# Low parts of a third of the early weight chunks by accumulating transfers, and 128-column causal matmuls in the attention

## The chip, the core and the metric

The kernel runs on one core of a Trainium2 chip. The metric is the device time of one execution in microseconds (us). The kernel before was run three times: the median is 706.12 us, the lowest 705.9 and the highest 706.37. One further execution was profiled; it took 705.1 us.

## The reference, cut to what matters

The program is a decoder trunk of two layers on 256 tokens with a model width of 1024, all in float32. In each layer one projection gives the attention's q, k, v and gate, an indexer's q, k and head weights, the input and gate of a recurrence, and two merge gates. The indexer's scores pick 64 causal keys for each query, and softmax attention runs over these.

```python
h = rmsnorm(x, norm_g[l])
proj = h @ w_in[l]
q, k, v, ga, iq, ik, iw, xr, gr, ma, mb = jnp.split(proj, offsets, axis=-1)
...
dots = jnp.einsum('bqhd,bsd->bqhs', iqb, ik)               # indexer
idx_score = jnp.einsum('bqh,bqhs->bqs', iwb, jax.nn.relu(dots))
idx_score = jnp.where(causal[None], idx_score, -jnp.inf)
_, sel = lax.top_k(idx_score, topk)
...
logits = jnp.einsum('bqhd,bqkhd->bhqk', qb, k_sel) * scale  # attention over the kept keys
p = jax.nn.softmax(jnp.where(valid[:, None], logits, -jnp.inf), axis=-1)
attn = jnp.einsum('bhqk,bqkhd->bqhd', p, v_sel)
y_a = (attn * jax.nn.silu(ga)) @ w_out_attn[l]
y_b = (hr * jax.nn.silu(gr)) @ w_out_rnn[l]                 # hr: the recurrence
x = x + (jax.nn.sigmoid(ma) * y_a + jax.nn.sigmoid(mb) * y_b) @ w_o[l]
```

A query attends to no key behind it, so for the first 128 queries only the first 128 keys count.

## The kernel before

The time is in the weights. All of them stand in one stream of 128x128 blocks in the order in which they are used; eight blocks make a chunk of 128x1024 numbers (512 KB), and 224 chunks are loaded as `raw` and two half chunks as `rah`, all from SyncE's queue. TensorE multiplies in fp32r, a format that holds fewer bits than float32, so every weight is split: `wh` is the chunk rounded to fp32r, `wl` is what the rounding lost, `raw - wh`. The activations are split alike (`hh` and `hl`), and `mm3` does three matmuls for each block: high by high, low by high, high by low. A chunk therefore makes 24 matmuls of 256 columns, or 12 of 512 where a projection is laid out by token (`v`, `ma`, `mb`, `yb`, `ya`). `wh` is a copy on ScalarE or, where the planner puts it there, on VectorE; `wl` is always a subtraction on VectorE (`chunk`, L556 to L572; the recorded line is that of the helpers `copy`, L480 and L482, and `sub`, L486). There are 4 buffers for `raw` and 6 pairs of `wh` and `wl`.

The order on each engine is not that of the code. `plan` lists the units of a layer in the order of the weight stream: the indexer's queries, then the recurrence with the light projections between, then for each pair of heads q, k, (v for four heads) and `attn`, then `yb`, `ya` and the output. Every operation is recorded with an estimated duration, and `Program.issue` then runs a simulated clock over all of them: for each engine `choose` takes the operation that can start first, and of several the one with the lowest priority number. On TensorE that number is the place in the recorded order plus a delay (`late`), so the indexer's `dots` and the attention's logits (`lg`), transposes (`ptp`) and products with v (`av`) are pushed behind later projections and fill in between their matmuls. On the other engines it is a due time that is counted back from TensorE's order. What comes out is fixed: each engine works through its list in order and waits at semaphores.

In the attention two blocks of 128 queries are handled as t = 0 and 1. `dots` (L876) and `logits` (L1082) let all matmuls run over 256 keys, though for t = 0 only the first 128 are read afterwards. `attend` (L1107) turns the three causal 128x128 blocks of the softmax weights, puts them behind 128 columns of zeros in `pth` and `ptl`, and multiplies with v: for both blocks of keys 256 columns, of which half are those zeros for the second block. `self.vt` holds the split v of four heads; it is made anew for the second four.

Of the kernel before, what the change touches and what calls it, by code (L numbers as in the profile page):

```python
# [20 lines left out]
L = 2  # L21
# [43 lines left out]
def plan(l):  # L65

    u = [("head",)]
    iq = [("iq", i) for i in range(8)]
    light = []
    for n, i in (("ga", 0), ("mb", 0), ("ga", 1), ("mb", 1), ("ga", 2), ("ma", 0), ("ga", 3), ("ma", 1)):  # L70
        light += [(n, 2 * i), (n, 2 * i + 1)] if n == "ga" else [(n, i, c) for c in range(4)]
    u += iq[3:NRAW]
    for i in range(NRAW, 8):
        u += light[:NMIX] + [iq[i]]
        light = light[NMIX:]
    for j in range(KR):
        u += [("xr", j), ("gr", j)]
        u += light[:2 if j % 3 == 0 else 1]
        light = light[2 if j % 3 == 0 else 1:]
        if j >= DELAY:  # L80
            u.append(("gate", j - DELAY))
    for j in range(KR - DELAY, KR):
        u += light[:2]
        light = light[2:]
        u.append(("gate", j))
    u += light
    for pr in range(4):
        u += [("q", 2 * pr), ("q", 2 * pr + 1), ("k", 2 * pr), ("k", 2 * pr + 1)]
        if pr % 2 == 0:
            u += [("v", pr // 2, c) for c in range(4)]  # L90
        u.append(("attn", pr))
    u += [("yb", n) for n in range(2)]
    if l == L - 1:
        return u + [("xt", 0), ("ya", 0), ("xt", 1), ("ya", 1), ("wt", 0), ("wt", 1)]
    u += [("ya", n) for n in range(2)]
    return (u + [("wo", m, 0, 4) for m in range(6)] + [("wo", m, 4, 8) for m in range(6)]
            + [("wo", m, 0, 8) for m in range(6, 8)])
# [48 lines left out]

NBLK = sum(len(unit_blocks(u)) for l in range(L) for u in plan(l))
NCH = -(-NBLK // 8)


class H:
# [57 lines left out]
def real(a):  # L209
    return a.ap() if isinstance(a, V) else a  # L210
# [12 lines left out]
TABS[AF.Sqrt] = ("sqrt",)  # L223
TABS[AF.Sin] = ("sin",)
PSUM_TAGS = ("pp", "pq", "pt")
ENGINES = ("pe", "act", "dve", "pool", "dma")
LATENCY = {"pe": 190.0, "act": 140.0, "dve": 130.0, "pool": 200.0, "dma": 2000.0}
TO_PE = 230.0
SWITCH = 1283.0

# [1 line left out]
class Program:  # L232
# [52 lines left out]
    def issue(self):  # L285
# [24 lines left out]
        for o in ops:  # L310
            if not o.need:
                enter(o)
        table = None
        order = []
        n = 0
        total = len(ops)
        pepos = 0.0
        while n < total:
# [19 lines left out]
            for h in o.new:  # L338
                k = (h.pool, h.tag)
                slots[k].pop(0)  # L340
                given[k][h.index] = True
                while nalloc[k] < len(given[k]) and given[k][nalloc[k]]:
                    nalloc[k] += 1
            o.start, o.end = s, s + cost
            free[o.eng] = o.end
            if o.eng == "pe":
# [47 lines left out]
    def choose(self, e, cand, free, slots, nalloc, given, table, pepos):  # L394

        best = None
        now = free[e]
        for o in cand:
            s = max(now, o.ready)
            if e != o.eng and max(free[o.eng], o.ready) < s + GAIN:  # L400
                continue
            ok = True
            for h in o.new:
                k = (h.pool, h.tag)
                fr = slots[k]
                ahead = min(h.index - sum(given[k][nalloc[k]:h.index]) - nalloc[k], KEEP.get(h.tag, 1000))
                if len(fr) <= ahead:
                    ok = False
                    break
                s = max(s, fr[0])  # L410
            if not ok:
                continue
            pr = o.prio[0]
            if e == "act" and o.tabs is not ANY and table not in o.tabs:
                pr += TABLE_LAG
                if o.prio[0] > pepos + URGENT:
                    s = max(s, o.ready + HOLD)
            key = (s if s > now else now, pr, o.no)
            if best is None or key < best[0]:
                best = (key, s, o)  # L420
        return None if best is None else (best[1], best[2])
# [2 lines left out]
RING = ("pp", "pq", "pt", "wh", "wl", "raw", "lt0", "lt1", "f2", "mx", "m8")  # L424
KEEP = {"r2": 6, "f1": 5, "f2": 1}
TABLE_LAG = 10000.0
URGENT = 8000.0
HOLD = 0.0
GAIN = 500.0
# [3 lines left out]
def trunk(ctx, tc, xT, pos, pre, par, fgb, wst, out):  # L433
# [78 lines left out]
              lambda: nc.tensor.matmul(real(o), real(w), real(m), start=start, stop=stop, skip_group_check=grp))  # L512

    def trans(o, i):
        pg.op("pe", 70, [o], [i, ident], lambda: nc.tensor.transpose(real(o), real(i), real(ident)))

    def load(o, src, cost, beside=False):

# [9 lines left out]
    class Stream:  # L528
# [23 lines left out]
        def chunk(self, c):  # L552
            if c not in self.parts:
# [11 lines left out]
                    return self.parts[c]  # L565
                wh = pg.tile(wp, "wh", [P, 1024], F32R, nm("wh"), WBUF)
                wl = pg.tile(wp, "wl", [P, 1024], F32R, nm("wl"), WBUF)
                copy(wh, raw)
                sub(wl, raw, wh.bitcast(F32))
                pg.shift = 0.0  # L570
                self.parts[c] = (wh, wl)
            return self.parts[c]  # L572
# [58 lines left out]
    pg.op("pool", 500, [ident], [], lambda: make_identity(nc, real(ident)))  # L631
    pts = []
    for i in range(2):
        ph = const(f"pth{i}", [512], F32R)
        pl = const(f"ptl{i}", [512], F32R)
        pset(ph.bitcast(F32)[:, 0:128], 0.0)
        pset(pl.bitcast(F32)[:, 0:128], 0.0)
        pts.append((ph, pl))

    def mm3(o, rhs, first, last, grp=False):  # L640
        wh, wl = ws.block()
# [143 lines left out]
    class Layer:  # L785
        def __init__(self, l, xg, norm):
# [4 lines left out]
            self.sga, self.sma, self.smb = {}, {}, {}  # L791
            self.xc, self.xs, self.rix, self.sy, self.g = {}, {}, {}, {}, {}
            self.rope = {}
            self.aT = []
            self.m = []
            self.banks = {}
# [74 lines left out]
        def dots(self, i, st, t):  # L871

            pg.late = LATE_DOTS
            ps = bank("pq", "dots")
            for a in range(2):
                w = st[a][:, t * P:t * P + P]  # L876
                mm(ps[:, a, :], w, self.kh, True, False)
                mm(ps[:, a, :], w, self.kl, False, True)
            pg.late = 0.0
            n = P * (t + 1)  # L880
            o = self.wk[t]
            rl = f2("rl")
            act(rl[:, :, :n], ps[:, :, :n], AF.Relu)
# [183 lines left out]
        def v(self, n, c):  # L1067
            ps = self.by_token("v", self.h[2 * c:2 * c + 2], c == 0, c == 3)
            if c == 3:
                self.vt = []  # L1070
                for t in range(2):
                    self.vt.append((r2("vh").join(), r2("vl").join()))
                    split(self.vt[t], ps[t])

        def attn(self, pr):
            pg.late = LATE_LOG
# [5 lines left out]
        def logits(self, hd):  # L1082
# [1 line left out]
            a = hd % 2  # L1084
            ps = bank("pq", "lg")
            for t in range(2):
                s = slice(t * P, t * P + P)
                mm(ps[:, t, :], qh[:, a, s], kh[:, a, :], True, False)
                mm(ps[:, t, :], qh[:, a, s], kl[:, a, :], False, False)
                mm(ps[:, t, :], ql[:, a, s], kh[:, a, :], False, True)  # L1090
            lts = []
            for t in range(2):
                n = P * (t + 1)
# [14 lines left out]
        def attend(self, hd, lts):  # L1108
            pg.late = LATE_LOG + LATE_TURN
            ps = bank("pt", "ptp").join()  # L1110
            for dst, lt, s in ((384, 1, 0), (128, 1, P), (256, 0, 0)):
                trans(ps[:, dst:dst + P], lts[lt][:, s:s + P])
            ph, pl = pts[hd % 2]
            act(ph[:, P:], ps[:, P:], AF.Copy)
            sub(pl[:, P:], ps[:, P:], ph.bitcast(F32)[:, P:])
            a = hd % 4
            pg.late = LATE_LOG + 2 * LATE_TURN
            ps = bank("pt", "av")[:, 0, :]
            n = 0
            for st in range(2):  # L1120
                vh, vl = self.vt[st]
                r = slice(256 - 256 * st, 512 - 256 * st)
                c = slice(a * P, a * P + P)
                for w, m in ((vh, ph), (vh, pl), (vl, ph)):
                    mm(ps, w[:, c], m[:, r], n == 0, n == 5)
                    n += 1
            of = f1("of")
            mul(of, ps, self.sga[hd])
# [191 lines left out]
```

## Time and profile before

| | |
|---|---|
| median of three runs | 706.12 us |
| the profiled execution | 705.1 us, of which its span 703.3 us |
| TensorE matmuls busy | 686.1 us (98%), 4720 instructions |
| VectorE busy | 602.6 us (86%) |
| ScalarE busy | 482.8 us (69%) |
| transfers of the weight queue | 124.44 MB, 56.5% of the 16 DMA engines' time |

All times below are of the one profiled execution and count from the start of its span. TensorE pipelines its matmuls: the duration of a row runs to the end of the last result and covers the next matmul's start, so a busy TensorE may still be slower than it could be. Its pace is the distance between the starts of two rows that follow each other. A number in brackets at a row's end is time in which the engine sat idle before it, with what ended that.

### The profile page before, as it was taken

To read this page: it belongs to the slowest core of one execution; us is meant where nothing else is said; L and a number is where in the kernel's file an instruction comes from. 1 tells how busy PE (TensorE), PEld (TensorE's weight loads), DVE (VectorE), ACT (ScalarE), POOL (GpSimd) and SP (SyncE) were. 2 spreads that over 40 slices of the span, in tenths; PEclk is the share of its full clock that TensorE was granted. 3 is DMA by queue.
4 is the path that set the end of the run, shared out by engine and by line. 5 is a ranking of instruction groups with operands and counts; after the bars stand their busy time and mean duration, and the time that the engine had idled before them with its cause. 6 is when DMAs were issued, how large, how long until landed. Compare 5 with 4: busy or idle time off the path is not lost.

```text
span 703.3 us, 12628 instructions
## 1 busy us (share of the span) xinstructions
PE 686.1 (98%) x4720; PEld 638.4 (91%) x4720; DVE 602.6 (86%) x1177; ACT 482.8 (69%) x775; POOL 6.4 (1%) x18
## 2 busy tenths in 40 slices
PE   7898999999999999999999999999999999999996
PEld 7898999999999998888999899999999898988885
DVE  7989999999897959857779997999989987796573
ACT  7996675799995748444558766588769765674433
POOL 0000000000000000000000000000000000000000
PEclk9999999999999999999999999999999999999999
DMA  8646566667756462655553655576666565535621
GB/s 292 195 157 211 159 197 201 203 189 220 223 177 189 149 192 75 205 180 179 173 173 111 213 178 163 177 220 207 210 205 185 182 190 163 180 101 171 195 73 60
DMA packets 38104, 125.24 MB, mean 178 GB/s; under 512 B 4892, under 2 KB 7260, under 8 KB 38044
## 3 DMA queue, kind: packets, MB, share of 16 engines
q1 hardware_dynamic: 38044, 124.44, 56.5%
q8 instruction: 37, 0.61, 0.3%
q14 instruction: 23, 0.19, 0.1%
HBM read 119.77 MB, written 1.05 MB: 172 GB/s over the span
## 4 chain that ended last, share of the span: by engine, by line
PE 82%; DVE 7%; ACT 6%; issue 2%; DMA 2%; SPq 0%; DVEq 0%; ACTq 0%
PE rps L512 14%; PE yb L512 9%; PE q L512 7%; PE k L512 7%; PE ops L512 6%; PE ma L512 6%; PE ya L512 6%; PE v L512 6%; PE gps L512 5%; PE ga L512 4%; PE mb L512 4%; DVE wl L486 2%; PE iq L512 2%; ACT wh L480 2%; PE lg L512 2%
## 5 line engine op out<-in xcount | busy, mean ns | idle before, releaser
L486 DVE TENSOR_TENSOR wl<-raw,wh 128x1024 fp32r<-128x1024 f32 x223 | 271.5, 1220 | 58.4 <-ACT wh L480 57.1
L480 ACT ACTIVATE wh<-raw 128x1024 fp32r<-128x1024 f32 x196 | 207.3, 1059 | 138.6 <-PE rps L512 21.4
L512 PE MATMUL rps<-hh,wh 128*128 128x256 f32 x352 | 99.5, 283 | 0.0
L512 PE MATMUL rps<-hl,wh 128*128 128x256 f32 x352 | 99.5, 283 | 0.0
L512 PE MATMUL rps<-hh,wl 128*128 128x256 f32 x352 | 99.5, 283 | 0.0
L512 PEld LDWEIGHTS rps<-hh,wl 128*128 128x128 f32 x352 | 67.4, 192 | 0.3
L512 PEld LDWEIGHTS rps<-hh,wh 128*128 128x128 f32 x352 | 67.3, 191 | 0.3
L512 PEld LDWEIGHTS rps<-hl,wh 128*128 128x128 f32 x352 | 67.4, 191 | 0.0
L512 PE MATMUL yb<-wh,g 128*128 128x512 f32 x176 | 59.0, 396 | 0.0
L512 PE MATMUL iq<-xg,wh 128*128 128x256 f32 x232 | 45.3, 285 | 0.0
L512 PE MATMUL ya<-wh,aT 128*128 128x512 f32 x128 | 40.8, 395 | 0.0
L512 PE MATMUL ga<-hh,wh 128*128 128x256 f32 x128 | 36.3, 283 | 2.0 <-DVE iwt L486 2.0
L512 PEld LDWEIGHTS iq<-xg,wh 128*128 128x128 f32 x232 | 37.4, 192 | 0.0
L512 PEld LDWEIGHTS yb<-wh,g 128*128 128x128 f32 x176 | 32.5, 188 | 5.3
L512 PE MATMUL q<-hh,wl 128*128 128x256 f32 x128 | 36.4, 284 | 0.0
L512 PE MATMUL q<-hh,wh 128*128 128x256 f32 x128 | 36.3, 284 | 0.0
L512 PE MATMUL ga<-hl,wh 128*128 128x256 f32 x128 | 36.3, 283 | 0.0
L512 PE MATMUL k<-hh,wl 128*128 128x256 f32 x128 | 36.3, 283 | 0.0
L512 PE MATMUL q<-hl,wh 128*128 128x256 f32 x128 | 36.2, 283 | 0.0
L512 PE MATMUL ga<-hh,wl 128*128 128x256 f32 x128 | 36.2, 283 | 0.0
L512 PE MATMUL k<-hh,wh 128*128 128x256 f32 x128 | 36.2, 283 | 0.0
L512 PE MATMUL k<-hl,wh 128*128 128x256 f32 x128 | 36.2, 283 | 0.0
(264 smaller groups left out, 1944.6 us busy)
## 6 DMA issues: line engine op xcount, KB each, us to landing
raw<-in_wst_dram SPq DMA_DIRECT2D x224, 512.0 KB, 4.0
xk<-xs SPq DMA_DIRECT2D x24, 48.0 KB, 3.5
out_dram<-z SPq DMA_DIRECT2D x4, 256.0 KB, 2.3
rah<-in_wst_dram SPq DMA_DIRECT2D x2, 256.0 KB
xr<-in_xT_dram SPq DMA_DIRECT2D x1, 512.0 KB
fg<-in_fgb_dram SPq DMA_DIRECT2D x2, 256.0 KB
xk<-xs SPq DMA_DIRECT2D x8, 40.0 KB
xf<-xs SPq DMA_DIRECT2D x2, 160.0 KB
```

Source lines behind the costliest of these rows:

```text
L480: lambda: nc.scalar.activation(real(o), real(i), AF.Copy),
L486: lambda: nc.vector.tensor_tensor(real(o), real(a), real(b), op=op))
L512: lambda: nc.tensor.matmul(real(o), real(w), real(m), start=start, stop=stop, skip_group_check=grp))
```

## The change

Two things are changed, and the planner's numbers with them. First, chunks 6, 9, 12 and so on of the stretch of each layer that lies ahead of the q projections (`SUMMED`, 38 chunks in all) get their `wl` in another way: ScalarE writes minus the rounded chunk into `wl`, and a transfer that GpSimd issues adds the chunk to it from HBM. `wh` is copied as before, and `raw` is still loaded. Second, for t = 0 the matmuls of `dots` and `logits` run over 128 keys, and in `attend` the second block of keys takes 128 columns; the zeros and the four instructions that set them go. That makes 160 matmuls narrower: 64 `dots`, 48 `lg` and 48 `av`. In the planner a matmul cannot take less than `ISSUE` unless wider ones ahead of it have left something over (`spare`), narrow ones are held back until there is, and a transpose is given a larger cost. The v projection of heads 4 to 7 is moved ahead, between the q and k projections of the second pair.

```diff
--- before.py
+++ after.py
@@ -86,8 +86,10 @@
         u += [("q", 2 * pr), ("q", 2 * pr + 1), ("k", 2 * pr), ("k", 2 * pr + 1)]
-        if pr % 2 == 0:
-            u += [("v", pr // 2, c) for c in range(4)]
+        if pr == 0:
+            u += [("v", 0, c) for c in range(4)]
+        if pr == 1:
+            u[-4:] = [w for c, w in enumerate(u[-4:]) for w in (("v", 1, c), w)]
         u.append(("attn", pr))
@@ -148,6 +150,20 @@
+def summed_chunks():
+    out, n = set(), 0
+    for l in range(L):
+        early = sum(len(unit_blocks(u)) for u in plan(l)[:plan(l).index(("q", 0))])
+        out.update(range(n // 8 + 6, (n + early) // 8, 3))
+        n += sum(len(unit_blocks(u)) for u in plan(l))
+    return out
+SUMMED = summed_chunks()
@@ -223,8 +239,8 @@
 PSUM_TAGS = ("pp", "pq", "pt")
-ENGINES = ("pe", "act", "dve", "pool", "dma")
-LATENCY = {"pe": 190.0, "act": 140.0, "dve": 130.0, "pool": 200.0, "dma": 2000.0}
+ENGINES = ("pe", "act", "dve", "pool", "dma", "sum")
+LATENCY = {"pe": 190.0, "act": 140.0, "dve": 130.0, "pool": 200.0, "dma": 2000.0, "sum": 3500.0}
 TO_PE = 230.0
@@ -341,6 +358,9 @@
                     nalloc[k] += 1
+            if o.eng == "pe":
+                cost = max(cost, ISSUE - self.spare)
+                self.spare = min(max(self.spare + cost - ISSUE, 0.0), SPARE)
             o.start, o.end = s, s + cost
@@ -415,6 +435,8 @@
                     s = max(s, o.ready + HOLD)
+            if e == "pe" and o.cost < ISSUE:
+                pr += -SHORT if self.spare >= ISSUE - o.cost - 5.0 else SHORT
             key = (s if s > now else now, pr, o.no)
@@ -424,6 +446,9 @@
 TABLE_LAG = 10000.0
+ISSUE = 110.0
+SPARE = 60.0
+SHORT = 6000.0
 URGENT = 8000.0
@@ -512,7 +537,7 @@
     def trans(o, i):
-        pg.op("pe", 70, [o], [i, ident], lambda: nc.tensor.transpose(real(o), real(i), real(ident)))
+        pg.op("pe", 112, [o], [i, ident], lambda: nc.tensor.transpose(real(o), real(i), real(ident)))
@@ -565,8 +590,15 @@
                 wl = pg.tile(wp, "wl", [P, 1024], F32R, nm("wl"), WBUF)
-                copy(wh, raw)
-                sub(wl, raw, wh.bitcast(F32))
+                if c in SUMMED:
+                    pg.op("act", 94 + 0.833 * 1024, [wl], [raw],
+                          lambda: nc.scalar.activation(real(wl), real(raw), AF.Copy, scale=-1.0))
+                    copy(wh, raw)
+                    pg.op("sum", 2000, [wl], [wl],
+                          lambda: nc.gpsimd.dma_start(real(wl), wst[c], accum_op=OP.add))
+                else:
+                    copy(wh, raw)
+                    sub(wl, raw, wh.bitcast(F32))
                 pg.shift = 0.0
@@ -631,11 +663,7 @@
     for i in range(2):
-        ph = const(f"pth{i}", [512], F32R)
-        pl = const(f"ptl{i}", [512], F32R)
-        pset(ph.bitcast(F32)[:, 0:128], 0.0)
-        pset(pl.bitcast(F32)[:, 0:128], 0.0)
-        pts.append((ph, pl))
+        pts.append((const(f"pth{i}", [384], F32R), const(f"ptl{i}", [384], F32R)))
@@ -872,12 +901,12 @@
             ps = bank("pq", "dots")
+            n = P * (t + 1)
             for a in range(2):
                 w = st[a][:, t * P:t * P + P]
-                mm(ps[:, a, :], w, self.kh, True, False)
-                mm(ps[:, a, :], w, self.kl, False, True)
+                mm(ps[:, a, :n], w, self.kh[:, :n], True, False)
+                mm(ps[:, a, :n], w, self.kl[:, :n], False, True)
             pg.late = 0.0
-            n = P * (t + 1)
             o = self.wk[t]
@@ -1067,10 +1096,9 @@
             if c == 3:
-                self.vt = []
+                self.vt[n] = [(r2("vh").join(), r2("vl").join()) for _ in range(2)]
                 for t in range(2):
-                    self.vt.append((r2("vh").join(), r2("vl").join()))
-                    split(self.vt[t], ps[t])
+                    split(self.vt[n][t], ps[t])
@@ -1084,10 +1112,10 @@
             for t in range(2):
-                s = slice(t * P, t * P + P)
-                mm(ps[:, t, :], qh[:, a, s], kh[:, a, :], True, False)
-                mm(ps[:, t, :], qh[:, a, s], kl[:, a, :], False, False)
-                mm(ps[:, t, :], ql[:, a, s], kh[:, a, :], False, True)
+                s, n = slice(t * P, t * P + P), P * (t + 1)
+                mm(ps[:, t, :n], qh[:, a, s], kh[:, a, :n], True, False)
+                mm(ps[:, t, :n], qh[:, a, s], kl[:, a, :n], False, False)
+                mm(ps[:, t, :n], ql[:, a, s], kh[:, a, :n], False, True)
             lts = []
@@ -1108,21 +1136,21 @@
             ps = bank("pt", "ptp").join()
-            for dst, lt, s in ((384, 1, 0), (128, 1, P), (256, 0, 0)):
+            for dst, lt, s in ((2 * P, 1, 0), (0, 1, P), (P, 0, 0)):
                 trans(ps[:, dst:dst + P], lts[lt][:, s:s + P])
+            ps = ps[:, :3 * P]
             ph, pl = pts[hd % 2]
-            act(ph[:, P:], ps[:, P:], AF.Copy)
-            sub(pl[:, P:], ps[:, P:], ph.bitcast(F32)[:, P:])
+            act(ph, ps, AF.Copy)
+            sub(pl, ps, ph.bitcast(F32))
             a = hd % 4
             n = 0
-            for st in range(2):
-                vh, vl = self.vt[st]
-                r = slice(256 - 256 * st, 512 - 256 * st)
+            for st, r in ((0, slice(P, 3 * P)), (1, slice(0, P))):
+                vh, vl = self.vt[hd // 4][st]
                 c = slice(a * P, a * P + P)
                 for w, m in ((vh, ph), (vh, pl), (vl, ph)):
-                    mm(ps, w[:, c], m[:, r], n == 0, n == 5)
+                    mm(ps[:, st * P:], w[:, c], m[:, r], n == 0, n == 5)
                     n += 1
```

VectorE, in the first 25 us, from the scaled unit matrices of the norm (`dg`) on; `wl` and `wh` are the parts of weight chunks, `ang` and `kk` belong to the rotary tables, `hf` to the normed input. Before:

```order
L501 TENSOR_SCALAR dg_267<-ident_76,sd_234 128x128
L501 TENSOR_SCALAR kk_270<-ang_258 128x256
L486 TENSOR_TENSOR wl_277<-raw_207,wh_253 128x1024
L501 TENSOR_SCALAR kk_270<-kk_270 128x256
L486 TENSOR_TENSOR wl_293<-raw_225,wh_274 128x1024
L505 SCALAR_TENSOR_TENSOR ang_258<-kk_270,ang_258 128x256
L486 TENSOR_TENSOR wl_316<-raw_240,wh_296 128x1024
L505 SCALAR_TENSOR_TENSOR ang_258<-kk_270,ang_258 128x256
L486 TENSOR_TENSOR wl_339<-raw_264,wh_319 128x1024
L505 SCALAR_TENSOR_TENSOR ang_258<-kk_270,ang_258 128x256
L505 SCALAR_TENSOR_TENSOR hf_362<-head_72,rstd_305 128x256
L505 SCALAR_TENSOR_TENSOR ang_258<-kk_270,ang_258 128x256
```

and in the changed kernel:

```order
L526 TENSOR_SCALAR dg_259<-ident_76,sd_226 128x128
L526 TENSOR_SCALAR kk_262<-ang_250 128x256
L507 CAST wh_268<-raw_217 128x1024
L511 TENSOR_TENSOR wl_275<-raw_199,wh_245 128x1024
L526 TENSOR_SCALAR kk_262<-kk_262 128x256
L530 SCALAR_TENSOR_TENSOR ang_250<-kk_262,ang_250 128x256 x2
L511 TENSOR_TENSOR wl_310<-raw_232,wh_288 128x1024
L530 SCALAR_TENSOR_TENSOR ang_250<-kk_262,ang_250 128x256
L511 TENSOR_TENSOR wl_333<-raw_256,wh_313 128x1024
L530 SCALAR_TENSOR_TENSOR ang_250<-kk_262,ang_250 128x256
```

The chunk that was `raw_225` is now `raw_217`: VectorE copies its high part (`CAST`) and has no subtraction for it; its low part is row 22 of ScalarE and the first transfer of GpSimd (`DMA wl_266<-in_wst_dram`).

TensorE, where the indexer's first `dots` are filled in, in the changed kernel; `mb` and `rps` are projections of 512 and 256 columns:

```order
L537 MATMUL mb_737<-wh_535,hh_379 128x512
L537 MATMUL dots_746<-kh_695,iqs_554 128x128
L537 MATMUL mb_737<-wl_551,hh_379 128x512
L537 MATMUL mb_737<-wh_535,hl_392 128x512
L537 MATMUL mb_737<-wh_584,hh_399 128x512
L537 MATMUL dots_746<-kl_735,iqs_554 128x128
L537 MATMUL mb_737<-wl_602,hh_399 128x512
L537 MATMUL dots_746<-kh_695,iqs_562 128x128
L537 MATMUL mb_737<-wh_584,hl_449 128x512
L537 MATMUL dots_746<-kl_735,iqs_562 128x128
```

and a little later:

```order
L537 MATMUL dots_780<-kl_735,iqs_554 128x128
L537 MATMUL rps_782<-hh_379,wh_614 128x256
L537 MATMUL rps_782<-hh_379,wl_596 128x256
L537 MATMUL rps_782<-hl_392,wh_614 128x256
L537 MATMUL rps_782<-hh_399,wh_614 128x256
L537 MATMUL dots_780<-kh_695,iqs_562 128x128
L537 MATMUL rps_782<-hh_399,wl_596 128x256
L537 MATMUL rps_782<-hl_449,wh_614 128x256
L537 MATMUL rps_782<-hh_399,wh_614 128x256
L537 MATMUL rps_782<-hh_399,wl_596 128x256
L537 MATMUL dots_780<-kl_735,iqs_562 128x128
```

Before, each `dots` stood behind one `rps` matmul and had 256 columns. Now the first of these narrow ones stand behind a 512-column matmul, and the later ones behind every fourth 256-column one.

TensorE in the attention, the first pair's logits (`lg`): before, between the k projection's matmuls of the second pair,

```order
L512 MATMUL lg_3020<-kh_2856,qh_2802 128x256
L512 MATMUL k_2973<-hh_426,wh_2843 128x256
L512 MATMUL lg_3020<-kl_2866,qh_2802 128x256
L512 MATMUL k_2973<-hh_426,wl_2859 128x256
L512 MATMUL lg_3020<-kh_2856,ql_2818 128x256
L512 MATMUL k_2973<-hl_441,wh_2843 128x256
L512 MATMUL lg_3020<-kh_2856,qh_2802 128x256
L512 MATMUL k_2973<-hh_436,wh_2871 128x256
L512 MATMUL lg_3020<-kl_2866,qh_2802 128x256
```

and in the changed kernel between those of q and of the second v projection:

```order
L537 MATMUL lg_2958<-kh_2867,ql_2829 128x128
L537 MATMUL q_2943<-hh_468,wl_2846 128x256
L537 MATMUL q_2943<-hl_482,wh_2834 128x256
L537 MATMUL q_2943<-hh_468,wh_2834 128x256
L537 MATMUL q_2943<-hh_468,wl_2846 128x256
L537 MATMUL lg_2977<-kh_2867,qh_2813 128x128
L537 MATMUL q_2943<-hl_482,wh_2834 128x256
L537 MATMUL v_2919<-wh_2834,hh_399 128x512
L537 MATMUL lg_2977<-kl_2877,qh_2813 128x128
L537 MATMUL v_2919<-wl_2846,hh_399 128x512
L537 MATMUL lg_2977<-kh_2867,ql_2829 128x128
L537 MATMUL v_2919<-wh_2834,hl_449 128x512
```

The narrow ones (t = 0) are spread out until the 512-column matmuls of `v` come; the 256-column ones (t = 1) follow further down.

## Rows read from the trace of the kernel before

**Rows 1.** The page: busy us of each engine, its share of the span, instructions

```profile
PE 686.1 (98%) x4720; PEld 638.4 (91%) x4720; DVE 602.6 (86%) x1177; ACT 482.8 (69%) x775; POOL 6.4 (1%) x18
```

**Rows 2.** TensorE's waits after its start: releaser, us in total, times, longest

```profile
PE ga L512 <- DVE iwt L486: 2.0, 1, 2.0
PE dots L512 <- DVE kl L486: 1.5, 1, 1.5
PE dots L512 <- ACT rl L473: 1.5, 2, 1.1
PE mb L512 <- DVE ga L486: 0.7, 1, 0.7
```

**Rows 3.** Windows: length, each engine's busy us, clock, DMA share, GB/s

```profile
0.00:20.00 20.00, 14.87 (x108) 14.82 (x109) 15.50 (x33) 15.72 (x26) 1.28 (x10) 1.00 0.82 283
20.00:40.00 20.00, 18.02 (x150) 17.84 (x150) 18.08 (x31) 19.33 (x30) 0.00 (x0) 1.00 0.63 207
100.00:200.00 100.00, 100.00 (x728) 95.09 (x728) 94.77 (x208) 83.06 (x137) 1.63 (x2) 1.00 0.67 203
```

**Rows 4.** Timeline of TensorE: start us, us, then the instruction; 256 and 512 columns

```profile
226.08 0.28 PE L512 MATMUL k<-hh,wl 128*128 128x256 f32 x1
226.20 0.28 PE L512 MATMUL k<-hl,wh 128*128 128x256 f32 x1
...
308.26 0.39 PE L512 MATMUL ya<-wl,aT 128*128 128x512 f32 x1
308.49 0.61 PE L512 MATMUL ya<-wh,aT 128*128 128x512 f32 x2
308.94 0.39 PE L512 MATMUL ya<-wl,aT 128*128 128x512 f32 x1
```

**Rows 5.** Timeline of TensorE's weight loads behind narrow matmuls and behind a stall

```profile
13.11 0.98 PEld L512 LDWEIGHTS nps<-ones,nsq 128*128 128x128 f32 x8
...
30.82 0.19 PEld L512 LDWEIGHTS ga<-hh,wh 128*128 128x128 f32 x1 [2.16 <-ACT sw L473]
30.93 0.19 PEld L512 LDWEIGHTS ga<-hh,wl 128*128 128x128 f32 x1
...
292.68 0.14 PEld L515 LDWEIGHTS ptp<-ident,lt 128*128 128x128 f32 x1
292.89 0.30 PEld L512 LDWEIGHTS yb<-wh,g 128*128 128x128 f32 x2
```

**Rows 6.** Timeline of TensorE around the transpose that belongs to these last loads

```profile
292.57 0.48 PE L512 MATMUL yb<-wl,g 128*128 128x512 f32 x1
292.89 0.27 PE L515 MATMUL ptp<-ident,lt 128*128 128x128 f32 x1
```

**Rows 7.** Groups by form: busy us, mean ns; idle before

```profile
L486 DVE TENSOR_TENSOR wl<-raw,wh 128x1024 fp32r<-128x1024 f32 x223 | 271.5, 1220 | 58.4 <-ACT wh L480 57.1
L482 DVE CAST wh<-raw 128x1024 fp32r<-128x1024 f32 x27 | 18.6, 690 | 6.1 <-PE iq L512 1.7 <-PE ga L512 1.3 <-PE rps L512 1.3
L480 ACT ACTIVATE wh<-raw 128x1024 fp32r<-128x1024 f32 x196 | 207.3, 1059 | 138.6 <-PE rps L512 21.4 <-PE ya L512 20.3 <-PE yb L512 19.2
```

**Rows 8.** Timeline of VectorE and TensorE at the first `dots`

```profile
56.22 1.21 DVE L486 TENSOR_TENSOR wl<-raw,wh 128x1024 fp32r<-128x1024 f32 x1
57.46 0.42 DVE L486 TENSOR_TENSOR kl<-ikr,kh 64x256 fp32r<-64x256 f32 x1
...
57.93 0.39 PE L512 MATMUL dots<-kl,iqs 128*128 128x256 f32 x1 [1.55 <-DVE kl L486]
```

**Rows 9.** Transfers: the weight queue's share, and issues with KB and us to landing

```profile
q1 hardware_dynamic: 38044, 124.44, 56.5%
...
raw<-in_wst_dram SPq DMA_DIRECT2D x224, 512.0 KB, 4.0
```

**Rows 10.** Timeline of ScalarE and TensorE: an early chunk, split and used

```profile
15.19 2.00 ACT L480 ACTIVATE wh<-raw 128x1024 fp32r<-128x1024 f32 x2
...
25.95 0.28 PE L512 MATMUL iq<-xg,wl 128*128 128x256 f32 x1
```

More of the change, by code (lines that the diff above doesn't have):

```diff
@@ L313, in issue @@
         table = None
+        self.spare = 0.0
         order = []
@@ L793, in __init__ @@
             self.rope = {}
+            self.vt = {}
             self.aT = []
```

## The prediction

> **What bounds the kernel now.** I read the engines' busy time first: TensorE is busy for 98% of the span, VectorE for 86%, ScalarE for 69% [rows 1]. The table of windows comes next: from 100 to 200 us TensorE's matmuls leave no gap at the full granted clock of 1.00 (2.4 GHz), while VectorE is busy for 94.77 of 100 us and the DMA engines for 0.67 [rows 3]. So the pace is TensorE's, with VectorE close behind it. Third, TensorE's waits: apart from its first matmul it waits 2.0 + 1.5 + 1.5 + 0.7 = 5.7 us in all, for VectorE or ScalarE [rows 2]. These waits lie early in each layer, where VectorE and ScalarE both run at over 90% from 20 to 40 us [rows 3]. One shows its cause: the last `kl`, for which TensorE idles 1.55 us, stands on VectorE behind a `wl` of 1.21 us [rows 8]. The change can thus give something in two ways: less work in TensorE's row, and fewer of these waits.
>
> **TensorE's pace, and what 128 columns are worth.** Two matmuls of 256 columns start 0.12 us apart; three of 512 take 0.68 us, so 0.227 each [rows 4]. 256 more columns cost 0.107 us; if columns alone counted, a matmul of 128 would take 0.12 - 0.0535 = 0.0665. But each matmul also has a weight load. Eight loads for matmuls of a single column stand (0.98 - 0.19) / 7 = 0.113 us apart, and behind a stall, with fp32r weights as in the projections, the second load starts 0.11 after the first [rows 5]. So a load needs 0.11 us, however little is multiplied. The question is whether a 512-column matmul in front hides this. The nearest case is a transpose of 128 columns: its weights were loaded from 292.68, while a 512-column matmul still ran; the transpose starts at 292.89 [rows 6]. The next load starts only then, at 292.89, and the load after it, which starts when the matmul behind the transpose really runs, at 292.89 + 0.30 - 0.19 = 293.00 [rows 5]. So the narrow matmul took 0.11 although a wide one stood ahead of it: one set of weights is loaded ahead, not two.
>
> I therefore take 0.111 for a narrow matmul: 160 x (0.120 - 0.111) = 1.4 us. The bounds are 160 x 0.0535 = 8.6 us, if columns alone count, and 0; a loss I exclude, since no load in the rows behind a narrow matmul is further off than 0.113. The value is the one nearest to the load rows. The Trainium skill ("TensorE: Matmul & The Clock Gate", section "LDWEIGHTS (loading the stationary operand)") gives a load as columns / 1.2 ns, which is 107 ns for 128 columns, and the trace agrees at 110 to 113. The same page (section "Back-to-back issue gap") speaks against my value: it gives about 81 ns per matmul for a stream of loads and matmuls of 128 columns. By that the gain would be an estimated 160 x 0.039 = 6.2 us; no row here shows such a pace.
>
> **The waits.** In 38 of the 224 chunks VectorE loses the subtraction of 1.22 us. By the lists of the engines it gets 23 more copies of `wh` at 0.69, and ScalarE gets 38 negations (1.06 each, as its copies, the same size [rows 7]) for 23 copies fewer. VectorE: -38 x 1.22 + 23 x 0.69 = -30.5 us; ScalarE: 15 x 1.06 = +15.9 us. For each wait of [rows 2] I compare what stands ahead on the two engines. Ahead of the `iwt` that releases `ga`, VectorE has four `wl` in place of five, plus two copies: some 0.8 us less, so 2.0 becomes about 1.2. Between `iwt` and the second `kl` five `wl` stand in place of nine, -4.9 us, with some 2.5 us of other work moved in: the 1.5 us go. Of the remaining 2.2 us (`rl` and `mb`) I let 1.6 go, since chunks 6 to 18 and their likes in the second layer have by then taken several subtractions away. Sum 0.8 + 1.5 + 1.6 = 3.9 us; bounds 0 and 5.7.
>
> **What I cost at nothing, and its cover.** An accumulating transfer is not in the trace. A plain load of 512 KB lands 4.0 us after its issue [rows 9]; I bound the accumulating one by 4.0 and by twice that, 8.0, since it has two operands to read. The first has least time: its negation stands on ScalarE where a chunk's copy ended at 17.2, and the low part of its place in the stream is first used at 25.95 [rows 10], 8.8 us later. Later ones have more, since six pairs of buffers at 24 x 0.12 = 2.9 us per chunk allow over 10 us. If the first is late, TensorE waits among `iq`, but the 1.2 us that remain before `ga` absorb it. GpSimd is busy for 6.4 us [rows 1]; its list now mixes the transfers with the index masks, so a mask that waits for VectorE holds the transfers behind it, and TensorE would wait for their `wl`; the 10 us cover that. SyncE's loads of `raw` stay as many. The second v projection moves ahead with the same 48 matmuls and holds four more small buffers; were one missing, a PSUM bank would come free late, at a price like the 0.7 us of `mb`. The zeros were set where nothing waited.
>
> **Sum.** 1.4 + 3.9 = 5.3 us off the profiled execution's 705.1 (span 703.3 and 1.8 around it): 699.8. The median is 1.0 above that execution, so I forecast 700.8. What is late next, where the waits go, is TensorE's own row. With the ends 0 and 5.7 of the waits and the narrow matmuls at 1.4 this case runs from 699.0 to 704.7; I give it 698.5 to 704.
>
> **Rivals.** *A, a wide matmul does hide the load.* Against it stands the transpose of [rows 5, 6]; for it, that a transpose is not fp32r and may be a special case. In the new order only 58 of the 160 stand right behind a 512-column matmul. If those alone cost 0.0665, they give 58 x 0.0535 = 3.1 us and the others 0.9, so 700.8 - 2.6 = 698.2; if all do, 8.6, so 693.6. By the Trainium skill's 81 ns (the same page) the estimate is 696.0.
>
> *B, slower: the transfers fill the DMA engines.* The weight queue took 56.5% of 703.3 us for 124.44 MB, 1.67 us of all sixteen engines for each 512 KB [rows 9]. From 100 to 200 us 33 us are free [rows 3]. In 100 us TensorE uses 100 / 2.88 = 34.7 chunks, so 11.6 accumulating ones: the point from which this decides is 33 / 11.6 = 2.85 us each. At the price of a plain load nothing happens. If reading the destination too doubles it to 3.34, each is 0.49 too much, 38 x 0.49 = 18.6 us, and `raw` comes late: 706.1 + 18.6 - 5.3 = 719.4. Against it: the share overstates what is used, for at 0.82 the engines moved 283 GB/s and at 0.67 only 203 [rows 3], 345 against 303 at a full share. By bytes, 142 GB/s would be free, 14.2 MB in 100 us, where doubled transfers need 12.2. The Trainium skill ("Collectives: The Full Stack", section "The bandwidth ceiling: the fold count and why AG ≠ RS ≠ AR") holds that adding in the DMA engine costs nothing in itself but needs two reads, so half the rate; that is the doubled price, and no run here shows it yet.
>
> *C, VectorE's relief comes to nothing.* ScalarE is busy for 19.33 us from 20 to 40 us [rows 3] and gets more work there; TensorE then waits for ScalarE or a late `wl` in place of VectorE. Only the 1.4 us stay: 704.7. For it speaks that two of the waits already name ScalarE [rows 2].
>
> **How the numbers follow.** Chances: forecast 0.54, A 0.13, B 0.20, C 0.13. The range is 696 to 709: it leaves out A's far end (0.06) and most of B (0.13). About 0.2%, or 1.4 us, is what a measurement of this kernel can tell from no change, so faster means under 704.7. The forecast, A and half of C are faster: 0.54 + 0.13 + 0.065 = 0.735. The other half of C and a tenth of B are the same: 0.085. The rest of B is slower: 0.18. The forecast's own range stands above, since B has the other sign.
>
> **What would show it.** In the changed profile a narrow `dots`, `lg` or `av` should start 0.11 us before what follows it, behind a wide matmul as elsewhere; 0.07 would mean A. TensorE's waits should sum to about 1.8 us, with `dots <- kl` gone. GpSimd's transfers should land in 4 to 8 us, and the DMA share from 100 to 200 us should rise to between 0.86 (0.67 + 11.6 x 1.67 / 100) and 1. Waits of TensorE for a transfer into `wl`, or of ScalarE for `raw` well above before, would mean B. TensorE's waits at 5 us or more would mean C. I am wrong altogether if TensorE idles in the attention, where I expect no new wait.

## The result and the profile after

The changed kernel takes 714.58 us (median of four runs, 712.28 to 715.37); the kernel before, run beside it, 706.25 (705.9 to 706.8). The ratio is 1.0112, 95% interval 1.0087 to 1.0137. The change costs 8.3 us where the prediction had a gain of 5.3, and 714.58 lies outside the range.

The page after the change, of one execution of 715.37 us (the longest of the four): span, busy time of each engine, DMA queues, transfers (issues, KB each, median us to landing).

```profile
span 713.6 us, 12732 instructions
PE 691.4 (97%) x4720; PEld 642.3 (90%) x4720; DVE 576.8 (81%) x1164; ACT 496.6 (70%) x789; POOL 41.9 (6%) x52
...
q1 hardware_dynamic: 38044, 124.44, 54.1%
q0 software_dynamic: 5472, 19.93, 15.8%
...
raw<-in_wst_dram SPq DMA_DIRECT2D x224, 512.0 KB, 4.9
wl<-in_wst_dram POOLq DMA_DIRECT2D x38, 512.0 KB, 8.1
```

Against [rows 1], VectorE is relieved of 25.8 us and ScalarE has 13.8 more, much as predicted; yet the span is 10.3 us longer. The adding transfers land after 8.1 us, and plain loads take 4.9 where they took 4.0 [rows 9]. An adding transfer holds all sixteen engines for 15.8% x 713.6 / 38 = 2.97 us.

Where did it go? TensorE's waits after its start, and below them ScalarE's for the chunks that it copies (us in total, times, longest); for the chunks that it negates it waits 2.0 us more:

```profile
PE ga L537 <- DVE iwt L511: 3.4, 1, 3.4
PE dots L537 <- ACT sw L498: 2.9, 1, 2.9
PE mb L537 <- ACT kh L505: 2.4, 1, 2.4
PE mb L537 <- DVE iqr L511: 0.9, 1, 0.9
PE iq L537 <- DMA wl<-in_wst_dram: 0.8, 1, 0.8
PE dots L537 <- DVE kl L511: 0.4, 1, 0.4
...
ACT wh L505 <- DMA raw<-in_wst_dram: 6.6, 3, 3.3
```

TensorE's sum to 10.8 us against 5.7 [rows 2], and all lie before 60 us or from 400 to 406 us: at the start of a layer, up to its `dots`. The windows show such a place, whole and in halves, and the middle of the layer:

```profile
20.00:40.00 20.00, 15.82 (x118) 15.45 (x117) 14.99 (x27) 15.93 (x23) 1.73 (x2) 0.91 0.74 210
20.00:30.00 10.00, 9.18 (x77) 8.98 (x76) 5.41 (x11) 6.08 (x10) 0.87 (x1) 1.00 1.00 280
30.00:40.00 10.00, 6.64 (x44) 6.47 (x43) 9.58 (x17) 9.85 (x14) 0.86 (x1) 0.83 0.48 140
100.00:200.00 100.00, 100.00 (x731) 95.27 (x731) 85.60 (x190) 82.00 (x134) 12.53 (x14) 1.00 0.94 264
```

From 100 to 200 us the DMA engines are nearly full, at 0.94, and TensorE loses nothing. From 20 to 40 us it does 118 matmuls in place of the 150 of [rows 3]. The share there is 0.74 on average, but 1.00 in the first half, where the load comes late, and 0.48 in the second, where TensorE stands. So a full DMA engine alone is not the harm; a late transfer in a tight place is. ScalarE's timeline and then the chain of waits show one:

```profile
23.89 0.59 ACT L498 ACTIVATE sw<-iq 32x512 f32<-32x512 f32 x1
27.80 1.06 ACT L505 ACTIVATE wh<-raw 128x1024 fp32r<-128x1024 f32 x1 [3.32 <-DMA raw<-in_wst_dram]
```

```profile
18.90 8.82 DMA raw<-in_wst_dram
...
27.80 1.06 ACT wh L505
28.86 0.31 ACT kk L498
29.17 0.52 ACT hh L505
```

A plain load, issued as its buffer came free at 18.9, took 8.82 us. ScalarE works in order, so `hh` stood behind the copy of that chunk, VectorE waited 4.59 us for `hh`, and TensorE 3.4 us at `ga`. Not all of these 3.4 us are the late load's: with the same order and 8 columns for each transfer (e2 below) `ga` waits 1.2 us, but in other orders without an adding transfer so early it waits 2.4 (e1), 2.9 (e6), 3.0 (e3) and 3.3 us (e7). At 384 us it happens again: a load takes 8.10 us, ScalarE idles for 2.77, and TensorE waits 2.9 us at `dots`. The transfers of two stretches there, by queue (packets, MB, share of the sixteen engines), first 384 to 388 us and then 388 to 392.3:

```profile
q0 software_dynamic: 107, 0.44, 68.9%
q1 hardware_dynamic: 78, 0.32, 27.3%
```

```profile
q1 hardware_dynamic: 427, 1.56, 89.9%
q0 software_dynamic: 37, 0.09, 10.2%
```

While an adding transfer runs it takes 69% of the engines' time and leaves the plain loads 0.32 MB in 4 us; without it they move 1.56 MB in 4.3. A load that starts beside it is held up while it runs: that of 18.90 us lands at 27.72, and the adding transfer issued at 18.01, which takes 9.5 us, at 27.5.

Then the clock, which costs as much as the waits. In three stretches it is granted at 0.50, the lower of the two levels (1.2 GHz; the third value from the end):

```profile
35.20:38.60 3.40, 3.40 (x18) 3.40 (x17) 3.04 (x6) 3.38 (x5) 0.08 (x1) 0.50 0.38 151
59.10:62.50 3.40, 2.99 (x8) 2.45 (x9) 2.83 (x5) 3.35 (x5) 0.86 (x1) 0.50 0.55 108
403.80:410.60 6.80, 6.17 (x18) 4.92 (x19) 6.42 (x15) 4.54 (x9) 0.86 (x1) 0.50 0.74 187
```

Each begins in, or just behind, one of the long waits: 3.4 us at `ga`, 2.4 at `mb`, 2.9 at `dots`. In the profiled execution before, with waits of up to 2.0 us, the clock stayed at 1.00 until the last matmul. The third stretch:

```profile
404.02 0.45 PE L537 MATMUL dots<-kh,iqs 128*128 128x128 f32 x1 [2.88 <-ACT sw L498]
...
406.32 0.73 PE L537 MATMUL mb<-wh,hh 128*128 128x512 f32 x1
406.85 0.31 PE L537 MATMUL dots<-kl,iqs 128*128 128x128 f32 x1
406.96 0.73 PE L537 MATMUL mb<-wl,hh 128*128 128x512 f32 x1
```

A wide and a narrow matmul take 0.64 us there where they take 0.34 at the full clock (below).

I sum it by the starts of all 4720 matmuls, less 0.12, 0.227 or 0.11 us for each by its width: the rest is 11.0 us before and 23.0 after. The 12 us more, less 1.6 for narrower matmuls, give 10.4; the span grew by 10.3. Of the 12 us, 5.1 are longer waits (10.8 less 5.7), and 5.7 lie between the matmuls of the three stretches at the lower clock (1.5, 1.5 and 2.7). About 1.2 are left unassigned.

The narrow matmuls themselves, in the attention behind wide ones:

```profile
277.37 0.40 PE L537 MATMUL yb<-wl,g 128*128 128x512 f32 x1
277.60 0.22 PE L537 MATMUL lg<-kh,qh 128*128 128x128 f32 x1
277.66 0.45 PE L537 MATMUL yb<-wh,g 128*128 128x512 f32 x1
277.94 0.22 PE L537 MATMUL lg<-kh,qh 128*128 128x128 f32 x1
...
283.77 0.28 PE L537 MATMUL av<-ptl,vh 128*128 128x128 f32 x1
283.88 0.28 PE L537 MATMUL av<-pth,vl 128*128 128x128 f32 x1
283.99 0.44 PE L537 MATMUL yb<-wh,g 128*128 128x512 f32 x1
```

Narrow ones in a row start 0.11 apart. A narrow and a wide one start 0.34 apart (277.60 to 277.94): 0.34 - 0.227 = 0.11 again. What a narrow start gains behind a wide one, the next loses.

### The profile page after: what moved, and what is told of

Its sections match the earlier page's. It is cut to its first block, busy times and chain, and to the rows that moved or that the text cites. A ratio compares the mean times of both kernels' runs of the same rounds, so it can differ in the third digit from the quotient of the medians.

```text
span 713.6 us, 12732 instructions
## 1 busy us (share of the span) xinstructions
PE 691.4 (97%) x4720; PEld 642.3 (90%) x4720; DVE 576.8 (81%) x1164; ACT 496.6 (70%) x789; POOL 41.9 (6%) x52
## 3 DMA queue, kind: packets, MB, share of 16 engines
q0 software_dynamic: 5472, 19.93, 15.8%
## 4 chain that ended last, share of the span: by engine, by line
PE 88%; DMA 4%; ACT 4%; DVE 2%; issue 1%; SPq 0%; ACTq 0%; DVEq 0%
PE rps L537 16%; PE yb L537 9%; PE q L537 7%; PE k L537 6%; PE ops L537 6%; PE ma L537 6%; PE v L537 6%; PE ya L537 6%; PE mb L537 6%; PE ga L537 5%; PE gps L537 5%; DMA raw<-in_wst_dram 4%; PE iq L537 2%; PE dots L537 2%; PE lg L537 1%
## 5 line engine op out<-in xcount | busy, mean ns | idle before, releaser
L511 DVE TENSOR_TENSOR wl<-raw,wh 128x1024 fp32r<-128x1024 f32 x185 | 225.8, 1221 | 65.4 <-ACT wh L505 63.8
L505 ACT ACTIVATE wh<-raw 128x1024 fp32r<-128x1024 f32 x173 | 183.1, 1058 | 117.4 <-PE ya L537 19.6
L598 POOL DMA_DIRECT2D wl<-in_wst_dram x38 | 34.1, 896 | 467.5 <-ACT wl L595 220.1
L595 ACT ACTIVATE wl<-raw 128x1024 fp32r<-128x1024 f32 x38 | 40.1, 1055 | 15.0 <-PE rps L537 7.7
L507 DVE CAST wh<-raw 128x1024 fp32r<-128x1024 f32 x50 | 34.7, 694 | 17.8 <-PE rps L537 10.3
```

Source lines behind the costliest of these rows:

```text
L505: lambda: nc.scalar.activation(real(o), real(i), AF.Copy),
L507: lambda: nc.vector.tensor_copy(real(o), real(i))))
L511: lambda: nc.vector.tensor_tensor(real(o), real(a), real(b), op=op))
L595: lambda: nc.scalar.activation(real(wl), real(raw), AF.Copy, scale=-1.0))
L598: lambda: nc.gpsimd.dma_start(real(wl), wst[c], accum_op=OP.add))
```

## The experiments

The theory: an adding transfer in a tight place makes the plain load beside it late, ScalarE stands at the copy that wants it, and TensorE at what is queued behind that. The rivals: (1) the new order of the matmuls does it, (2) ScalarE's negations do, (3) all transfers together fill the DMA engines. Times are medians; the ratio to the kernel before, run beside each, has its 95% interval. The last two columns are of the one profiled execution: TensorE's waits after its start, and what its matmuls lost in stretches at the lower clock, both in us and summed as above (before: 5.7 and 0; the changed kernel: 10.8 and 5.7).

| run | us | ratio | waits | lower clock |
|---|---|---|---|---|
| e1 no sums | 705.53 | 0.9992 (0.9983 to 1.0) | 7.0 | 0 |
| e2 sums of 8 columns | 707.1 | 1.0005 (0.9997 to 1.0014) | 6.6 | 1.6 |
| e3 sums from the 18th chunk | 712.99 | 1.0097 (1.0082 to 1.0112) | 10.2 | 4.6 |
| e4 sums alone | 715.27 | 1.0134 (1.0116 to 1.0152) | 9.9 | 4.2 |
| e5 plain transfers | 709.22 | 1.0038 (1.0024 to 1.0052) | 7.8 | 4.6 |
| e6 sums from the 27th chunk | 705.49 | 0.9992 (0.9983 to 1.0001) | 6.1 | 1.5 |
| e7 narrow matmuls alone | 704.56 | 0.9977 (0.9968 to 0.9986) | 6.1 | 1.5 |
| e8 after, five `raw` | 709.15 | 1.005 (1.0035 to 1.0065) | 7.6 | 3.4 |
| e9 e7, five `raw` | 703.72 | 0.9964 (0.9951 to 0.9976) | 5.1 | 0 |
| e10 e1, five `raw` | 704.75 | 0.9982 (0.9973 to 0.9991) | 5.7 | 1.5 |

**e1: the sums off.**

```diff
-SUMMED = summed_chunks()
+SUMMED = set()
```

> No accumulating transfers (the set of summed chunks is empty); the 128-column matmuls, the new place of the v units and the planner's new rules stay as in the changed kernel. Theory (an accumulating transfer near the start of a layer makes the plain load beside it late, ScalarE stands at the copy that wants that load, and the matmul engine at what is queued behind the copy): 703.5 to 706 us, at most 1.4 us under before, since the narrow matmuls took 160 x 0.009 us off; ScalarE's waits for raw fall from 6.6 us to about 1.7, no stretch of 20 us under a granted clock of 0.97, and the excess of the matmul engine's busy time over 0.12/0.227/0.11 us a matmul falls from 23 us to about 11. Rival 1 (the planner's new order of the matmuls makes the stalls, sums or not): 711 us or more, with the stalls at 30, 53 to 57 and 400 us still there.

705.53 us: the loss goes with the sums, and rival 1 falls as the cause of it. The clock's mark held (1.00 up to the last matmul), and the rest beyond 0.12, 0.227 or 0.11 us a matmul fell to 12.8 us. One mark failed: ScalarE's waits for `raw` stayed at 7.3 us in total. What fell is the longest, from 3.3 to 1.8 us:

```profile
ACT wh L505 <- DMA raw<-in_wst_dram: 7.3, 6, 1.8
```

**e2: the same order without the bytes.**

```diff
-nc.gpsimd.dma_start(real(wl), wst[c], accum_op=OP.add)
+nc.gpsimd.dma_start(real(wl)[:, 0:8], wst[c][:, 0:8], accum_op=OP.add)
```

> The changed kernel with each accumulating transfer cut from 1024 columns to 8 of each partition, so that the other columns of wl stay the negated raw (the low part is left out there). Every instruction of every engine stays where it was; only the bytes of the 38 transfers go. Theory: 701 to 705 us, since the loads beside them are no longer late while VectorE stays relieved of 38 subtractions; ScalarE's waits for raw at most 2.5 us. Rival 1 (the order): 712 to 716, as the order is the same. Rival 2 (ScalarE's 38 negations at 0.95 us and the wait for GpSimd's issue, not the bytes): 710 or more.

707.1 us: 7.5 of the 9.1 us between e1 and the changed kernel are the bytes. In the profiled executions, with the same order, the bytes make 4.2 us of waits and 4.1 us of lower clock, the 8.3 us by which the spans differ (713.6 and 705.3). The time under e1 that I expected from VectorE's relief (701 to 705 us) did not come; it is 1.6 us more. TensorE's waits:

```profile
PE mb L537 <- ACT kh L505: 2.5, 1, 2.5
PE ga L537 <- DVE iwt L511: 1.2, 1, 1.2
PE dots L537 <- DVE kl L511: 0.8, 1, 0.8
PE dots L537 <- ACT sw L498: 0.7, 1, 0.7
PE dots L537 <- ACT rl L498: 0.7, 1, 0.7
PE mb L537 <- DVE iqr L511: 0.7, 1, 0.7
```

`ga` waits 1.2 us as predicted; but the sum is 6.6 us, since ScalarE, which has the work that VectorE lost, is now late with `kh`. That is no more than e1's 7.0. What e2 has over e1 is the clock: from 50 to 60 us, behind the wait for `kh`, it is granted at 0.83 in place of 1.00, and 1.6 us go there. Since e1 also has another order on every engine, rivals 1 and 2 together are worth these 1.6 us, not the size of the loss; which of them it is was not taken apart.

**e3: the first four sums of each layer left out.**

```diff
-range(n // 8 + 6, (n + early) // 8, 3)
+range(n // 8 + 18, (n + early) // 8, 3)
```

> The first four summed chunks of each layer are converted on VectorE again (chunks 18, 21, ... 60 and 130, 133, ... 172 stay summed: 30 of 38 transfers). Theory (only the few tight places near the start of each layer cost anything): 703 to 705.5 us, with the DMA share between 100 and 200 us still above 0.88 and the clock at 0.98 or more in every 20 us. Rival 3 (all transfers together fill the DMA engines, the loss grows with their count): 30/38 of the loss of 8.3 us stays on top of the 1.4 us gained, so 711 us or more. Rival 1 (the order): 711 or more.

712.99 us: my expectation fell, its mark for the clock too (0.83 from 30 to 40 us, behind 3.0 us at `ga`, before any adding transfer has run), and rival 3's bound held. The chain shows why: the first adding transfers now run beside the loads that `dots` needs, whose `rl` stands behind a blocked copy. In the second layer a load from 400.46 us took 8.31.

```profile
57.68 7.65 DMA raw<-in_wst_dram
...
66.40 0.38 ACT rl L498
66.77 0.04 issue
66.82 0.33 PE dots L537
```

So the tight stretch reaches to the end of `dots`, beyond the four chunks that I had left out. It needed e6 to tell this from rival 3.

**e4: the sums alone.** The 38 sums put into the kernel before, its matmuls and the rules for them as they were.

```diff
+SUMMED = summed_chunks()
...
-                copy(wh, raw)
-                sub(wl, raw, wh.bitcast(F32))
+                if c in SUMMED:
...
+                          lambda: nc.gpsimd.dma_start(real(wl), wst[c], accum_op=OP.add))
```

> The kernel before with the 38 accumulating transfers alone: no narrow matmuls, no new place for v, none of the planner's new matmul rules. Theory: the transfers alone carry the loss: 710 to 717 us, with raw late (ScalarE's waits for raw above 4 us) in the first 60 us. Rival 1 (the order): 700.5 to 706.5, before's time with or without the relief of VectorE.

715.27 us: the sums alone carry the whole loss. ScalarE waits 4.3 us for `raw` in the first 60 us.

**e5: plain transfers in their place.**

```diff
-nc.gpsimd.dma_start(real(wl), wst[c], accum_op=OP.add)
+nc.gpsimd.dma_start(real(wl), wst[c].bitcast(F32R))
```

> The changed kernel with the 38 transfers of GpSimd's queue made plain ones: the same 512 KB from the same place, written over wl instead of added to it (wl then holds the whole weight, so the low part is left out). The order on every engine stays. Theory A (the bytes of any second load in the tight places delay raw): half way or more of the loss over the cut transfers' 707.1 us remains, 709.5 to 714 us, with ScalarE's waits for raw above 4 us. Theory B (it is the addition, which takes about twice the DMA engines' time of a plain load): 706 to 709 us, transfers landing in about 5 us instead of 8.1, DMA time of that queue near 9% of the span instead of 15.8%.

709.22 us, between the ranges of both, with 28% of the loss over e2 left where A wanted half:

```profile
q0 software_dynamic: 5472, 19.93, 9.0%
...
raw<-in_wst_dram SPq DMA_DIRECT2D x224, 512.0 KB, 4.4
wl<-in_wst_dram POOLq DMA_DIRECT2D x38, 512.0 KB, 6.0
```

The bytes as such cost 2.1 us over e2, the adding 5.4 more. The ten runs go from 705.71 us, at a mean granted clock of 0.999, to 710.26 at 0.990, so these prices hold for the medians. In the profiled one (710.22) the waits are 1.2 us above e2's and the lower clock costs 3.0 more. A plain transfer holds the engines for 9.0% x 708.4 / 38 = 1.68 us (span 708.4); the adding one takes 1.77 times that.

**e6: the sums only behind `dots`.**

```diff
-range(n // 8 + 6, (n + early) // 8, 3)
+range(n // 8 + 27, (n + early) // 8, 3)
```

> Summed chunks only from the 27th of each layer on (27 to 60 and 139 to 172, 24 of 38 transfers), so that the first one is issued behind the dots stage of its layer (behind about 65 and 410 us). Theory (bytes hurt only where the matmul engine has no weights ahead, which are the stretches up to the end of dots): 704.5 to 707 us, no more than without sums, with raw still late in the middle of the layer (its transfers 6 us and longer) and the matmul engine not noticing. Rival 3 (count of transfers): 24/38 of the loss of 9 us, 710 us or more.

705.49 us, as without sums, although 24 of 38 transfers stay. The window and the transfers from 100 to 200 us:

```profile
100.00:200.00 100.00, 100.00 (x728) 95.11 (x727) 90.82 (x212) 82.71 (x136) 11.37 (x13) 1.00 0.92 262
```

```profile
raw<-in_wst_dram SPq DMA_DIRECT2D x36, 512.0 KB, 5.8
wl<-in_wst_dram POOLq DMA_DIRECT2D x10, 512.0 KB, 8.4
```

`raw` takes 5.8 us there (I expected 6 or more) and TensorE loses nothing. Rival 3 falls: place decides, not count. Nor is anything gained: VectorE's relief is worth nothing where TensorE does not wait.

**e7: the narrow matmuls alone.** From the changed kernel, the sums, the place of v and the rules on short matmuls taken back:

```diff
...
-            if e == "pe" and o.cost < ISSUE:
-                pr += -SHORT if self.spare >= ISSUE - o.cost - 5.0 else SHORT
...
```

> The kernel before with the 128-column matmuls alone (the 384-column turn of the attention goes with them): no sums, v where it was, the planner without the rules on short matmuls. By the rows of before and after 160 matmuls fall from 0.120 to 0.111 us, so 704.5 to 705.5 us if the order of before, and with it its 5.7 us of waits, stays; if the planner's new rules and the place of v are worth something by themselves it is slower than 705.5 us, which the same kernel with them took.

704.56 us, faster than both kernels. The new planner rules and place of v are not needed: e1, which has them, took 1 us more, though the intervals touch.

**e8: the changed kernel with one more buffer for `raw`.**

```diff
-F1 = 22
+F1 = 21
-RAWS = 4
+RAWS = 5
```

> The changed kernel with five buffers for raw instead of four (and 21 instead of 22 buffers of 256 columns, to make room). Theory (raw is late because the load was issued only as a buffer came free and then ran beside an accumulating transfer): one more load in flight brings part of it back, 706 to 712 us, with ScalarE's waits for raw under 5 us. Rival (the DMA engines are simply full in those stretches, so that one more load in flight only shares the same bandwidth): 712.5 to 716 us, raw landing later than the 4.9 us of the changed kernel.

709.15 us: 5.4 of the 8.3 us come back although every byte is still moved. `raw` still lands in 4.9 us, but it is issued earlier (the twelfth load at 22.7 us in place of 31.9), and ScalarE hardly waits for it. The planner also orders anew for five buffers; what that does was not tested by itself. ScalarE's waits:

```profile
ACT wh L505 <- DMA raw<-in_wst_dram: 0.6, 2, 0.4
```

**e9 and e10: the fifth buffer without sums** (the edit of e8 in e7 and in e1).

> The narrow matmuls alone (no sums, v and the planner as before), with five buffers for raw and 21 of 256 columns. Theory (what is left to gain at the two tight places is a raw that comes late, 7.2 us of ScalarE's waits in the kernel with the narrow matmuls alone): 700.5 to 704 us, below the 704.56 us that it took with four buffers, ScalarE's waits for raw under 2.5 us, and the matmul engine's wait at ga (3.3 us) under 2. Rival (the conversions bound those places, not the loads, or the early loads come earlier only by taking bandwidth from what the start needs): 704 to 707 us.

> The changed kernel without sums, with five buffers for raw and 21 of 256 columns. Against the changed kernel with sums and five buffers (709.15 us) it shows what the sums cost when raw is not late: theory (ScalarE's 38 negations, 1.6 us by the cut transfers, and one transfer late by 1.4 us): 703 to 706 us, so that 3 to 6 us remain for the sums. Rival (the sums cost something only by making raw late): 708 to 710 us, as with sums.

e9 takes 703.72 us, the best time here; all its runs (703.02 to 703.92) lie under those of e7 (704.02 to 705.13), though the intervals of the ratios overlap. TensorE's wait at `ga` is 1.6 us (3.3 in e7), and no stretch at the lower clock follows, where e7 lost 1.5 us. e10 takes 704.75: with five buffers the sums still cost 4.4 us (709.15 less 704.75). Up to 1.6 of these could be what e2 had over e1, and in e8 TensorE waits 1.4 us for a late sum; the rest was not taken apart.

## Why the prediction was wrong

- **The narrow matmuls: right.** 0.11 us each, and e7 gained 1.6 us (1.4 predicted). Rival A falls by the rows at 277 us: its sign, a start 0.07 us before what follows, is there (277.60 to 277.66), but the next start is late by as much, so that sign could not tell. The 81 ns of the Trainium skill ("TensorE: Matmul & The Clock Gate", section "Back-to-back issue gap") are not reached: fp32r matmuls of 128 columns start 110 ns apart.
- **The waits, -3.9 us: wrong.** The single terms were fair (`ga` to 1.2 us, shown by e2), but I took them off as though nothing came in their place. With the bytes gone e2 has 6.6 us of waits against 5.7: C, relief for nothing. The step that failed is "I let 1.6 go": ScalarE, at 19.33 of 20 us [rows 3], was given 15.9 us more, and the sum charged nothing for it. Kernels without any sums have waits of 5.1 to 7.0 us (e1, e7, e9, e10), so e2's 6.6 is neither gain nor loss.
- **"What I cost at nothing, and its cover": the step that made the sign wrong.** I compared the transfer's landing with its own deadline, 8.0 against 8.8 us. That was nearly right at the median, 8.1 us; the first took 9.5, and TensorE waited 0.8 us for it. But "SyncE's loads of `raw` stay as many" counted them and not their time. One that runs beside an adding transfer took up to 8.82 us at the start of the first layer, against a median of 4.0 before, and ScalarE, in order, passes that on to all behind it. The runs price it: 7.5 us for the bytes (e1, e2), of which 5.4 are the adding (e5); 5.4 come back with one more buffer (e8).
- **Rival B: the right resource, the wrong place.** Its break-even of 2.85 us is just passed (2.97), and the share from 100 to 200 us is 0.94, within my 0.86 to 1. But a share near 1 cost nothing there. It cost at the start of a layer, where the weights ahead are few (0.96 over the late load, 18.9 to 27.8 us). I worked it out from the middle of a layer and took it as an average, so its time (719.4) was too high, its chance too low, and the range left its near part out. The Trainium skill ("Collectives: The Full Stack", section "The bandwidth ceiling: the fold count and why AG ≠ RS ≠ AR") gives a collective that adds, reading two sources, half the rate of one that copies; e5 against the changed kernel gives 1.77 times the engines' time, so the trace roughly agrees.
- **The clock** was in no term. It stayed at 1.00 before, and fell behind the new stalls; three stretches at half lost 5.7 us, more than the 5.1 us by which the waits themselves grew. The prediction charged a wait at its length alone; here the two together came to about twice the growth of the waits.

## What to carry to other kernels

A transfer that is hidden itself can still delay those beside it: ask for each load it overlaps what waits for that load, and what stands in order behind. Ask it in the stretch where the least is prefetched; an average share says nothing there, and the same transfers cost nothing once weights are ahead. Read the granted clock behind each stall: here what followed the stalls cost as much as the stalls. Moving work between two engines that are both full there gains nothing; a buffer more, which starts the load earlier, did.

## What the runs showed of the hardware

- In one stretch beside an adding transfer (384 to 388 us) plain loads got 27% of the engines' time; with little beside them (388 to 392.3 us), 90%. Per us of all sixteen engines the adding transfer moved 0.44 / (0.689 x 4.0) = 0.16 MB (384 to 388 us), plain loads 1.56 / (0.899 x 4.3) = 0.40 (388 to 392.3 us).
- All stretches at the lower clock up to the last matmul begin in, or just behind, one or two waits of TensorE, but not every wait is followed by one: 1.7 us at `dots` was (e10), 2.4 us at `ga` was not (e1). What decides is not shown.
- GpSimd needs 0.9 us to issue such a transfer, whatever its size: 897 ns for 8 columns (e2), 896 for 1024; a plain transfer of 1024 takes it 553 ns (e5). The row of e2:

```profile
L598 POOL DMA_DIRECT2D wl<-in_wst_dram x38 | 34.1, 897 | 459.1 <-ACT wl L595 250.6
```
